# Third down pass of an encoder block: unit 8 of three column groups in half-size products

## The chip, the cores and the metric

The kernel runs on one core of one Trainium2 chip. The metric is device time in microseconds (us). The time before is 2462.04 us, the median of three runs (2459.8 to 2468.41).

## The reference

One layer of a hybrid encoder in float32, with 512 tokens and width 2048. The part that matters here is the channel mixer at its end, and the norm behind it:

```python
x = x + g1 * (merged @ w_out[l])
h2 = rms_norm(x, norm2_w[l]) * (1.0 + sc2) + sh2
ff = (jax.nn.silu(h2 @ w_ffn_gate[l]) * (h2 @ w_ffn_up[l])) @ w_ffn_down[l]   # 5632 -> 2048
x = x + g2 * ff
return rms_norm(x, final_w)
```

`g2` is a row of 2048 gate values, the same for all tokens.

## The kernel before

Every float32 matrix product is made of three matmuls: each operand is split into a high and a low part (`split`: ScalarE copies the high part, VectorE subtracts it to give the low one), and high x high, high x low and low x high are summed in PSUM (`mm3`, lines 188 to 190).

The product with `w_ffn_down` runs over 5632 features, in 11 units of 512 features (4 feature tiles of 128). The 2048 output columns are taken in four groups `cc` of 512. The output of a group is 512 tokens x 512 columns. There are three down passes and a final pass:

- First pass: units 0 and 1, plain (`form2`).
- Second pass (`down_group` with units 2, 3, 4 in products and unit 5 plain), for each `cc`.
- Third pass (the loop near the end): units 6 and 7 in products, units 8 and 9 plain, for each `cc`. In `cc` 0 the two plain units come first (`lead`), in the others last (the `tail`).
- Final pass: unit 10, with the gate `g2` multiplied into its weights, the residual sum, and the final norm, by token tiles.

"In products" means that a unit's 512 x 512 x 512 block is computed by seven half-size products instead of eight, as in Strassen's scheme with Winograd's sums. `wforms` loads two raw weight tiles, makes four sums of 128 x 512 on VectorE (lines 696 to 699), and splits four tiles into the buffers `whl` (one of 128 x 512 and three of 128 x 1024; line 168 on ScalarE, line 170 on VectorE). `sforms` makes the same forms of a unit's activations, which it loads from `ff_d` in DRAM; they lie in one of three `slots` and are used by all four groups. The order of the products is `ORDER = (1, 2, 3, 5, 6, 7, 4)`, or `LATE` for the first unit of some groups. A plain unit (`plain` in `down_group`) splits two raw tiles and needs no sums; its split activations lie in an area `a0` or `a1` (`place`), 128 x 4096 each.

There are five raw buffers (`raw`) and five split buffers (`whl`). A unit in products takes two and four of them, a plain unit two and two. The weight loads go out on SyncE's queue (SP), each when its buffer is free again. The products of a group accumulate in the eight PSUM banks. When the units in products are done, the four banks that only they use go into the accumulator `acc` (lines 1466 to 1480) beside the tail, and the other four behind it (line 1485). `acc` is loaded from `acc_d` at the start of a group, by GpSimd's queue (POOL).

At the end of a group in the third pass, its gated sum is put into `due`, and is made behind unit 7 of the next group (`late`): line 1576 multiplies `acc` by `g2`, line 1577 adds the residual `xr`, each in two instructions of 128 x 1024. For `cc` 0 to 2 the sum is stored to `x2p_d`, and loaded again before the final pass (line 1557); the fourth stays in SBUF. The residual comes from `x2_d`, a DRAM tensor that the pass over `w_out` wrote, and is loaded by POOL group by group (line 1569), with the row of `g2` behind it (line 1570). In `cc` 3 POOL also loads the gate's rows for the final pass (`gf`, line 439, from `rows(wide2[0], g2_d)`), into the buffer of unit 7's forms. Unit 10's activations (`fl`) are loaded by POOL and split behind units 8 and 9 of `cc` 1.

The framework's planner sets the order of the instructions on each engine: by priority, which follows the program's order, and by its own estimate of when each is ready. So an engine's order differs from the program's. `tc.high_priority()` puts instructions forward; `behind` (`tc.keep_in_program_order`) keeps those it wraps in program order among each other. Each engine, and each queue, then works strictly in that order. `bg` holds generators such as `sforms`, which are taken a step further by `pump()` after each unit.

Of the kernel before, what the change touches and what calls it, by code (L numbers as in the profile page):

```python
# [14 lines left out]
F32 = mybir.dt.float32  # L15
# [5 lines left out]
P = 128  # L21
WARM = 12, 14
D = 2048
# [89 lines left out]
def encoder_block(ctx: ExitStack, tc, xp, xT, c, ada1_w, ada2_w, b_ada, norm1_w, w_in, q_norm_w, k_norm_w, bias,  # L113
# [1050 lines left out]

    x2_d = dram.tile([T, D], F32, name="x2d")
    mod["queue"] = nc.sync
# [18 lines left out]
    def residual(cc, g, ssq, eng, x, keep=None):  # L1185
        cs = slice(cc * 512, (cc + 1) * 512)

        def evac(i, b):
            o = io.tile([P, 512], F32, tag="io", name="ro")
            V.tensor_mul(o, b, g[:, cs])  # L1190
            eng.tensor_add(x(i, cc), x(i, cc), o)
            if ssq:
                square(x(i, cc), ssq[i][:, cc:cc + 1])
            if keep is not None:
                t0 = i // 2 * 256 + i % 2
                nc.sync.dma_start(keep[t0:t0 + 255:2, cs], x(i, cc))
        return evac
# [185 lines left out]

    def sforms(j, u):

        big, low = slots[j]
        e, o = (raw_tile("ffe") for _ in range(2))
        for a, r in enumerate((e, o)):
            nc.gpsimd.dma_start(r, ff_d[u][:, a * 1024:(a + 1) * 1024])
        sa = wq.tile([P, 1024], F32, tag="ta", name="sa", bufs=2)  # L1390
        sb = wq.tile([P, 1024], F32, tag="tb", name="sb", bufs=1)
# [125 lines left out]
    f0 = 40  # L1517
    xr = p_e.tile([P, 3072 + 64], F32, tag="s23072", name="xr")
    xo = [xr[:, :2048].rearrange("p (i n) -> p i n", i=NT)]
    fl = p_e.tile([P, 4096 + 64], F32R, tag="s24096", name="fl")  # L1520
    wl = {}
    x2p_d = [dram.tile([P, NT, 512], F32, name=f"x2pd{cc}") for cc in range(3)]
    sq3 = [small.tile([P, 4], F32, tag=f"sq{i}", name=f"sq3{i}", bufs=1) for i in range(NT)]
# [8 lines left out]
    def late(cc):  # L1532
        def behind(u):
            if cc == 0 and u == 8:
                while bg:
                    pump()
            if cc == 1 and u > 7:
                a = u - 8
                xl_pairs.append(ff_pair(10, a, [fl[:, a * 2048 + e * 1024:a * 2048 + (e + 1) * 1024] for e in range(2)],
                                        pin=tc.keep_in_program_order))  # L1540
            if u == 7 and due:
                due.pop()()
            if cc == 3 and u == 6:
# [20 lines left out]

    def factor(cc):
        return xr[:, 2048 + cc % 2 * 512:2560 + cc % 2 * 512]

    def residual_of(cc):
        nc.gpsimd.dma_start(xo[0], x2_d[:, cc * 512:(cc + 1) * 512].rearrange("(i p) d -> p i d", p=P))
        nc.gpsimd.dma_start(factor(cc), g2_d[cc].partition_broadcast(P).rearrange("p o d -> p (o d)"))  # L1570

    def gated_sum(cc, acc):
        to = xo[0] if cc < 3 else x2[3]
        for t in range(2):
            ts = slice(2 * t, 2 * t + 2)
            behind(V.tensor_mul(acc[:, ts], acc[:, ts], factor(cc).unsqueeze(1).to_broadcast([P, 2, 512])))
            behind(V.tensor_add(to[:, ts], xo[0][:, ts], acc[:, ts]))
        if cc < 3:
            nc.gpsimd.dma_start(x2p_d[cc], xo[0])
            residual_of(cc + 1)  # L1580

    residual_of(0)
    for cc in range(4):
        acc = acc_tile()
        nc.gpsimd.dma_start(acc, acc_d[cc])
        down_group(cc, (6, 7), cl, acc, late(cc), () if cc else (8, 9), late=cc > 1,
                   after_lead=cc == 1)
# [87 lines left out]
```

## Time and profile before

| | |
|---|---|
| median of three runs | 2462.04 us |
| profiled execution: its own time, its span | 2466.89 us, 2465.1 us |
| mean granted TensorE clock | 0.998 |
| second down pass, groups cc 1, 2, 3 | 38.86, 38.86, 42.74 us |
| third down pass, groups cc 0 to 3 | 40.20, 40.21, 40.21, 40.20 us |
| final pass, to the end of the span | 52.49 us |

PE is TensorE's matmuls and PEld its weight loads, DVE is VectorE, ACT ScalarE, POOL GpSimd, and SP SyncE. Times in a trace are counted from the start of the span. The stretches in the table begin and end where the timeline of PE shows a group's first matmul. A matmul's row gives 0.28 us for 128 x 256, but matmuls are pipelined: the distance from start to start, 0.11 us in the dense stretches, is what each costs. A wait is written as "who <- for whom: us in total, times, longest".

### The profile page before, as it was taken

How to read it: one execution, taken by the hardware profiler on the slowest of the kernel's cores; microseconds unless marked ns; L12 is line 12 of the kernel's file. 1: busy time of each engine (PE TensorE's matmuls, PEld its weight loads, DVE VectorE, ACT ScalarE, POOL GpSimd, SP SyncE). 2: the span in 40 equal slices, each digit the busy share in tenths (PEclk: the TensorE clock that was granted, in tenths of full speed). 3: DMA queues.
4: the chain of work that ended last, by engine and by line, in shares of the span. 5: the costliest groups of instructions: out<-in, count | busy, mean ns of one | idle time of the engine just before them, and what ended most of it. 6: DMA issues, size and time to landing. Idle time of an engine off the chain costs nothing.

```text
span 2465.1 us, 42367 instructions
## 1 busy us (share of the span) xinstructions
PE 2433.0 (99%) x17327; PEld 2279.4 (92%) x17327; DVE 2007.1 (81%) x2704; ACT 1069.2 (43%) x1466; POOL 150.8 (6%) x255
## 2 busy tenths in 40 slices
PE   8999999999999999999999999999999999999998
PEld 7888888999888888888999999999999998999997
DVE  7995778998677678667899889889899885687877
ACT  5223545544344523337744444444444454433333
POOL 0000000000011111111000000000000000000010
PEclk9999999999999999999999999999999999999999
DMA  9775232455767687867444454444454456546563
GB/s 354 291 261 159 82 98 83 146 180 187 245 206 235 214 297 248 301 204 230 137 154 154 140 163 153 127 156 154 138 171 139 136 189 223 187 155 231 192 246 126
DMA packets 213731, 461.77 MB, mean 187 GB/s; under 512 B 15153, under 2 KB 59553, under 8 KB 204833
## 3 DMA queue, kind: packets, MB, share of 16 engines
q1 hardware_dynamic: 174160, 309.76, 38.6%
q0 software_dynamic: 29872, 132.73, 15.8%
q10 hardware_dynamic: 9504, 16.58, 1.9%
q8 instruction: 136, 2.23, 0.4%
q14 instruction: 59, 0.48, 0.1%
HBM read 412.84 MB, written 46.17 MB: 186 GB/s over the span
## 4 chain that ended last, share of the span: by engine, by line
PE 71%; DVE 14%; issue 8%; DMA 5%; ACT 1%; POOL 0%; DVEq 0%; SPq 0%; POOLq 0%; ACTq 0%
PE mm L190 14%; PE mm L188 14%; PE mm L189 14%; PE S L188 6%; PE S L190 6%; PE S L189 6%; DVE whl L170 3%; PE Y L188 3%; PE Y L189 3%; PE Y L190 2%; DVE raw L524 2%; DMA raw<-in_w_down 2%; PE T L886 1%; DVE g_acc L631 1%; DMA raw<-in_w_in 1%
## 5 line engine op out<-in xcount | busy, mean ns | idle before, releaser
L168 ACT ACTIVATE whl<-raw 128x1024 fp32r<-128x1024 f32 (+1 forms) x483 | 453.7, 943 | 673.9 <-PE mm L190 292.2
L170 DVE TENSOR_TENSOR whl<-raw,whl 128x1024 fp32r<-128x1024 f32 (+1 forms) x483 | 517.5, 1086 | 124.0 <-ACT whl L168 123.7
L168 ACT ACTIVATE whl<-ta 128x1024 fp32r<-128x1024 f32 x124 | 131.4, 1060 | 182.6 <-PE mm L190 112.9
L168 ACT ACTIVATE whl<-tb 128x1024 fp32r<-128x1024 f32 x124 | 131.4, 1060 | 171.7 <-PE S L190 116.5
L170 DVE TENSOR_TENSOR whl<-ta,whl 128x1024 fp32r<-128x1024 f32 x124 | 151.3, 1220 | 41.8 <-ACT whl L168 41.5
L388 DVE SCALAR_TENSOR_TENSOR acc<-mw,cact,acc 128x1024 f32<-128x1024 f32 x124 | 158.8, 1281 | 19.6 <-DMA mw<-in_ada_w 19.3
L170 DVE TENSOR_TENSOR whl<-tb,whl 128x1024 fp32r<-128x1024 f32 x124 | 150.9, 1217 | 5.9 <-ACT whl L168 5.8
L366 POOL DMA_DIRECT2D mw<-in_ada_w x113 | 60.3, 534 | 1357.1 <-DVE acc L388 939.2
L697 DVE TENSOR_TENSOR ta<-raw,ta 128x512 f32<-128x512 f32 x124 | 85.2, 687 | 65.4 <-DMA raw<-in_w_down 27.2
L696 DVE TENSOR_TENSOR ta<-raw 128x512 f32<-128x512 f32 x124 | 85.3, 688 | 36.3 <-DMA raw<-in_w_down 33.8
L188 PE MATMUL mm<-x56h,whl 128*128 128x256 f32 x336 | 92.7, 276 | 0.3 <-DVE c L784 0.2
L189 PE MATMUL mm<-x56l,whl 128*128 128x256 f32 x336 | 92.4, 275 | 0.0
L190 PE MATMUL mm<-x56h,whl 128*128 128x256 f32 x336 | 92.4, 275 | 0.0
L188 PE MATMUL mm<-x3h,whl 128*128 128x256 f32 x320 | 88.1, 275 | 0.5 <-DVE c L782 0.5
L188 PE MATMUL mm<-whl,s 128*128 128x256 f32 x320 | 88.2, 276 | 0.0
L189 PE MATMUL mm<-whl,s 128*128 128x256 f32 x320 | 88.1, 275 | 0.0
L190 PE MATMUL mm<-x3h,whl 128*128 128x256 f32 x320 | 88.0, 275 | 0.0
L190 PE MATMUL mm<-whl,s 128*128 128x256 f32 x320 | 88.0, 275 | 0.0
L189 PE MATMUL mm<-x3l,whl 128*128 128x256 f32 x320 | 88.0, 275 | 0.0
L190 PE MATMUL S<-x56h,whl 128*128 128x256 f32 x320 | 88.0, 275 | 0.0
L188 PE MATMUL S<-x56h,whl 128*128 128x256 f32 x320 | 88.0, 275 | 0.0
L189 PE MATMUL S<-x56l,whl 128*128 128x256 f32 x320 | 88.0, 275 | 0.0
(1879 smaller groups left out, 8909.2 us busy)
## 6 DMA issues: line engine op xcount, KB each, us to landing
raw<-in_w_in SPq DMA_DIRECT2D x133, 512.0 KB, 4.7
mw<-in_ada_w POOLq DMA_DIRECT2D x113, 512.0 KB, 4.5
raw<-in_w_gate SPq DMA_DIRECT2D x92, 512.0 KB, 4.6
raw<-in_w_up SPq DMA_DIRECT2D x88, 512.0 KB, 4.6
raw<-in_w_down SPq DMA_DIRECT2D x88, 512.0 KB, 5.3
raw<-in_ada_w POOLq DMA_DIRECT2D x29, 1024.0 KB, 5.3
raw<-in_w_out SPq DMA_DIRECT2D x48, 512.0 KB, 5.4
ffd<-c SPq DMA_DIRECT2D x10, 1024.0 KB, 4.8
```

The source lines that it names most:

```text
L168: high = pin(S.activation(hi, src, AF.Copy))
L170: latest[:] = [high, pin(eng.tensor_sub(lo, src, hi))]
L188: nc.tensor.matmul(o, lh, rh, start=start, stop=False, **kw)
L189: nc.tensor.matmul(o, lh, rl, start=False, stop=False, **kw)
L190: nc.tensor.matmul(o, ll, rh, start=False, stop=stop, **kw)
L366: mod["queue"].dma_start(w, ada2_w[n * P:(n + 1) * P, :])
L388: behind(V.scalar_tensor_tensor(acc, part, cact[:, k:k + 1], acc, op0=ALU.mult, op1=ALU.add))
L524: V.scalar_tensor_tensor(raw, raw, 1.0, call, op0=ALU.mult, op1=ALU.mult, accum_out=y)
L631: V.tensor_add(acc, acc, b)
L696: V.tensor_sub(t1, b12, b11)
L697: V.tensor_sub(t2_, b22, t1)
L886: nc.tensor.transpose(tp[:, k * P:(k + 1) * P], e[:, k * P:(k + 1) * P], ident)
```

## The change

Unit 8 is computed in products in `cc` 1, 2 and 3, and stays plain in `cc` 0, where it leads. For that its activations are brought into forms once, in `cc` 0 behind unit 9: they are loaded into area `a1` by POOL in one transfer of 1 MB, not into raw buffers, and the sums and the forms' intermediate tiles lie there as well. The forms go into the third slot, which the second pass used for unit 4. What lay in that slot moves: the split activations of unit 10 (`fl`) go to `a1` behind the forms and are loaded by SP's queue; the residual tile `xr` is dropped, and the rows of `g2` get two small buffers.

The gated sum for `cc` 0 to 2 is no longer added on VectorE. The product goes to DRAM with a DMA that adds it to `x2_d` there, in two halves; `x2_d` is now eight tensors of 256 x 512, and the final pass loads it from there. For `cc` 3, VectorE adds into the loaded tile as before. The third gated sum, that of `cc` 2, is made behind unit 8 of `cc` 3 and not behind unit 7, behind the loads of the gate's rows. The weights of the final pass for `cc` 2 go to the third slot, and those for `cc` 3 stay in `a0`.

```diff
-    x2_d = dram.tile([T, D], F32, name="x2d")
+    x2_d = [[dram.tile([256, 512], F32, name=f"x2d{cc}{t}") for t in range(2)] for cc in range(4)]
...
-                nc.sync.dma_start(keep[t0:t0 + 255:2, cs], x(i, cc))
+                nc.sync.dma_start(keep[cc][i // 2][i % 2::2, :], x(i, cc))
...
-    def sforms(j, u):
+    def sforms(j, u, room=None):
...
+        else:
+            e, o, sa, sb = (room[:, n * 1024:(n + 1) * 1024] for n in range(4))
+            nc.gpsimd.dma_start(room[:, :2048], ff_d[u])
+            yield
...
+    def load_x2(to, cc):
+        for t in range(2):
+            nc.gpsimd.dma_start(to[:, 2 * t:2 * t + 2], x2_of(cc, t))
...
+            if cc == 0 and u == 9:
+                forms = sforms(2, 8, p_s.tile([P, 4096 + 64], F32, tag="a1", name="f8"))
+                next(forms)
+                bg.append(forms)
             if cc == 1 and u > 7:
                 a = u - 8
-                xl_pairs.append(ff_pair(10, a, [fl[:, ...] for e in range(2)], pin=tc.keep_in_program_order))
-            if u == 7 and due:
-                due.pop()()
+                if a == 0:
+                    fl.append(p_s.tile([P, 4096 + 64], F32R, tag="a1", name="fl"))
+                xl_pairs.append(ff_pair(10, a, [fl[0][:, ...] for e in range(2)], nc.sync, pin=tc.keep_in_program_order))
...
                 rows(wide2[0], g2_d)
+                load_x2(x2[3], 3)
+            if u == (8 if cc == 3 else 7) and due:
+                due.pop()()
...
                 for c in range(3):
-                    nc.gpsimd.dma_start(x2[c], x2p_d[c])
+                    load_x2(x2[c], c)
...
     def gated_sum(cc, acc):
-        to = xo[0] if cc < 3 else x2[3]
+        f = factors.pop(0).unsqueeze(1).to_broadcast([P, 2, 512])
         for t in range(2):
             ts = slice(2 * t, 2 * t + 2)
-            behind(V.tensor_mul(acc[:, ts], acc[:, ts], factor(cc).unsqueeze(1).to_broadcast([P, 2, 512])))
-            behind(V.tensor_add(to[:, ts], xo[0][:, ts], acc[:, ts]))
+            behind(V.tensor_mul(acc[:, ts], acc[:, ts], f))
+            if cc == 3:
+                behind(V.tensor_add(x2[3][:, ts], x2[3][:, ts], acc[:, ts]))
+            else:
+                nc.gpsimd.dma_start(x2_of(cc, t), acc[:, ts], accum_op=ALU.add)
         if cc < 3:
-            nc.gpsimd.dma_start(x2p_d[cc], xo[0])
-            residual_of(cc + 1)
+            factor_of(cc + 1)
...
-        down_group(cc, (6, 7), cl, acc, late(cc), () if cc else (8, 9), late=cc > 1,
+        down_group(cc, (6, 7, 8) if cc else (6, 7), {9: cl[9]} if cc else cl, acc, late(cc), () if cc else (8, 9), late=cc > 1,
                    after_lead=cc == 1)
...
-        wt = p_s.tile([P, 4096 + 64], F32R, tag=f"a{3 - cc}", name=f"w{cc}")
+        wt = (p_e if cc == 2 else p_s).tile([P, 4096 + 64], F32R, tag="s24096" if cc == 2 else "a0", name=f"w{cc}")
```

More of the change, by code (lines that the diff above doesn't have):

```diff
@@ L1194, in evac @@
             if keep is not None:
-                t0 = i // 2 * 256 + i % 2
-                nc.sync.dma_start(keep[t0:t0 + 255:2, cs], x(i, cc))
+                nc.sync.dma_start(keep[cc][i // 2][i % 2::2, :], x(i, cc))
         return evac
@@ L1382, in __getitem__ @@
             return tuple(Tokens(half(t)[:, :, q]) for t in self.pairs[j])
-    def sforms(j, u):
+    def sforms(j, u, room=None):
         big, low = slots[j]
[L1387 to L1391, printed above, removed]
+        if room is None:
+            e, o = (raw_tile("ffe") for _ in range(2))
+            for a, r in enumerate((e, o)):
+                nc.gpsimd.dma_start(r, ff_d[u][:, a * 1024:(a + 1) * 1024])
+            sa = wq.tile([P, 1024], F32, tag="ta", name="sa", bufs=2)
+            sb = wq.tile([P, 1024], F32, tag="tb", name="sb", bufs=1)
+        else:
+            e, o, sa, sb = (room[:, n * 1024:(n + 1) * 1024] for n in range(4))
+            nc.gpsimd.dma_start(room[:, :2048], ff_d[u])
+            yield
         a11, a21, a12, a22 = e[:, :512], e[:, 512:], o[:, :512], o[:, 512:]
@@ L1517, in encoder_block @@
     f0 = 40
[L1518 to L1522, printed above, removed]
+    fl, wl = [], {}
+    x2_of = lambda cc, t: x2_d[cc][t].rearrange("(i p) d -> p i d", p=P)
+    def load_x2(to, cc):
+        for t in range(2):
+            nc.gpsimd.dma_start(to[:, 2 * t:2 * t + 2], x2_of(cc, t))
     sq3 = [small.tile([P, 4], F32, tag=f"sq{i}", name=f"sq3{i}", bufs=1) for i in range(NT)]
@@ L1536, in behind @@
                     pump()
+            if cc == 0 and u == 9:
+                forms = sforms(2, 8, p_s.tile([P, 4096 + 64], F32, tag="a1", name="f8"))
+                next(forms)
+                bg.append(forms)
             if cc == 1 and u > 7:
                 a = u - 8
-                xl_pairs.append(ff_pair(10, a, [fl[:, a * 2048 + e * 1024:a * 2048 + (e + 1) * 1024] for e in range(2)],
-                                        pin=tc.keep_in_program_order))
-            if u == 7 and due:
-                due.pop()()
+                if a == 0:
+                    fl.append(p_s.tile([P, 4096 + 64], F32R, tag="a1", name="fl"))
+                xl_pairs.append(ff_pair(10, a, [fl[0][:, a * 2048 + e * 1024:a * 2048 + (e + 1) * 1024] for e in range(2)],
+                                        nc.sync, pin=tc.keep_in_program_order))
             if cc == 3 and u == 6:
@@ L1563, in encoder_block, with factor_of @@
     due = []
[L1565 to L1570, printed above, removed]
+    def factor_of(cc):
+        f = p_e.tile([P, 512], F32, tag="g2f", name="g2f", bufs=2)
+        nc.gpsimd.dma_start(f, g2_d[cc].partition_broadcast(P).rearrange("p o d -> p (o d)"))
+        factors.append(f)
     def gated_sum(cc, acc):
-        to = xo[0] if cc < 3 else x2[3]
+        f = factors.pop(0).unsqueeze(1).to_broadcast([P, 2, 512])
         for t in range(2):
             ts = slice(2 * t, 2 * t + 2)
-            behind(V.tensor_mul(acc[:, ts], acc[:, ts], factor(cc).unsqueeze(1).to_broadcast([P, 2, 512])))
-            behind(V.tensor_add(to[:, ts], xo[0][:, ts], acc[:, ts]))
+            behind(V.tensor_mul(acc[:, ts], acc[:, ts], f))
[3 more added lines that the diff above has]
+                nc.gpsimd.dma_start(x2_of(cc, t), acc[:, ts], accum_op=ALU.add)
         if cc < 3:
-            nc.gpsimd.dma_start(x2p_d[cc], xo[0])
-            residual_of(cc + 1)
-    residual_of(0)
+            factor_of(cc + 1)
+    factors = []
+    factor_of(0)
     for cc in range(4):
```

## The prediction

> **What bounds the kernel now.** First the page, for the engines' shares:
>
> ```profile
> PE 2433.0 (99%) x17327; PEld 2279.4 (92%) x17327; DVE 2007.1 (81%) x2704; ACT 1069.2 (43%) x1466; POOL 150.8 (6%) x255
> ```
>
> TensorE is busy 99%, so only less work on it, or fewer of its waits, can shorten the run. Next its waits from 1980 us to the end, where the change lies:
>
> ```profile
> PE S L189 <- DVE whl L170: 0.9, 1, 0.9
> PE S L188 <- ACT whl L168: 0.8, 1, 0.8
> PE mm L189 <- DVE w L170: 0.4, 1, 0.4
> ```
>
> 2.1 us of 485. Third, the table by stretch (columns: stretch, length, busy time of PE, PEld, DVE, ACT, POOL with counts, granted clock, DMA share, GB/s). I cut it where the timeline of PE shows a column group begin. The first three rows are the second down pass's groups cc 1 to 3, the next four the third pass's cc 0 to 3, then the final pass; the last two are a stretch across the third pass's first boundary, and one after a stall:
>
> ```profile
> 2131.33:2170.19 38.86, 38.86 (x350) 38.86 (x349) 27.43 (x36) 14.12 (x15) 1.07 (x2) 1.00 0.49 163
> 2170.19:2209.05 38.86, 38.86 (x350) 38.86 (x349) 29.34 (x39) 14.17 (x15) 2.13 (x4) 1.00 0.50 163
> 2209.05:2251.79 42.74, 41.02 (x350) 40.63 (x349) 36.58 (x46) 19.20 (x21) 5.02 (x9) 0.96 0.71 234
> 2251.79:2291.99 40.20, 40.20 (x362) 40.20 (x361) 30.56 (x40) 15.80 (x17) 1.61 (x3) 1.00 0.58 195
> 2291.99:2332.20 40.21, 40.21 (x363) 40.21 (x362) 34.10 (x42) 14.22 (x15) 2.91 (x5) 1.00 0.60 206
> 2332.20:2372.41 40.21, 40.21 (x362) 40.21 (x361) 32.02 (x40) 12.42 (x13) 2.38 (x4) 1.00 0.53 191
> 2372.41:2412.61 40.20, 40.20 (x362) 40.20 (x361) 29.34 (x32) 14.29 (x15) 5.02 (x9) 1.00 0.84 310
> 2412.61:2465.10 52.49, 42.23 (x206) 36.53 (x204) 41.86 (x80) 16.69 (x43) 0.00 (x0) 0.96 0.24 84
> ...
> 2228.40:2231.60 3.20, 3.20 (x18) 3.20 (x17) 2.39 (x4) 1.06 (x1) 0.53 (x1) 0.50 0.96 330
> ...
> 2266.50:2316.90 50.40, 50.40 (x454) 50.40 (x454) 48.42 (x61) 21.44 (x23) 3.75 (x7) 1.00 0.50 162
> ```
>
> The reader is to see three things. The four groups of the third pass are dense, 40.2 us each. A group of the second pass, which already has the shape that cc 1 to 3 are to get (three units in products, one plain), takes 38.86 us when dense; its fourth took 42.74. And VectorE is busy 48.42 of 50.40 us (96%) across the boundary from cc 0 to cc 1, just where the change adds to it.
>
> **The saving.** A plain unit is 4 feature tiles x 4 token tiles x 2 halves x 3 matmuls = 96; in products it is 7 x 2 x 2 x 3 = 84. cc 1, 2 and 3 lose 12 each, 36 in all. 40.21 / 360 matmuls is 0.1117 us each, so 36 x 0.1117 = 4.02 us; the rows agree, since 3 x (40.21 - 38.86) = 4.05. I take 4.0 us, 0.16% of the time.
>
> **What VectorE gets in return.**
>
> ```profile
> 2295.59 1.21 DVE L170 TENSOR_TENSOR whl<-tb,whl 128x1024 fp32r<-128x1024 f32 x1
> 2296.73 0.68 DVE L170 TENSOR_TENSOR whl<-raw,whl 128x512 fp32r<-128x512 f32 x1
> 2297.33 0.68 DVE L698 TENSOR_TENSOR tb<-raw 128x512 f32<-128x512 f32 x1
> 2297.93 0.68 DVE L699 TENSOR_TENSOR tb<-raw,ta 128x512 f32<-128x512 f32 x1
> 2298.53 1.22 DVE L170 TENSOR_TENSOR whl<-raw,whl 128x1024 fp32r<-128x1024 f32 x1
> ...
> 2301.94 1.21 DVE L1576 TENSOR_TENSOR acc<-acc,xr 128x1024 f32<-128x1024 f32 x1
> ...
> L1577 DVE TENSOR_TENSOR xr<-xr,acc 128x1024 f32<-128x1024 f32 x6 | 7.3, 1222 | 0.1
> ```
>
> Start to start, an operation of 128x1024 holds the engine 1.14 us and one of 128x512 0.60. Weights in forms: 4 sums x 0.60 + 0.60 + 3 x 1.14 = 6.4 us; a plain unit 2 x 1.14 = 2.3. That is +4.1 in each of three groups. Unit 8's activations in forms, once: the same 6.4. Removed: the adds of the first three gated sums, six by 1.14 = 6.8, since the DMA now accumulates; the last sum keeps its adds. Net 12.3 + 6.4 - 6.8 = +11.9 us on VectorE, against 160.8 - 126.0 = 34.8 us that it has free in the four groups. ScalarE's +2 and +4 splits fit into more than 24 us free in each group. So the total fits; the question is the place.
>
> The place is cc 1. TensorE reaches 2310.76 in the old cc 1, the start of unit 8, and the first gated multiplication begins at 2301.94. The fifth product of unit 8 comes 36 matmuls, 4.0 us, later: 2314.8. Before then, from 2301.94, VectorE has 12.9 us for two gated multiplications (2.3), unit 8's four weight sums and its first three splits (2.4 + 0.60 + 2 x 1.14 = 5.3) and the activation forms (6.4): 14.0 us. The evacuations that stand there now move behind unit 8. Short by 1.1 us. Lower bound 0, or below nothing if the queue is better packed than now (it has 2.0 us free in that 50.4 us stretch); upper bound: the forms are put ahead of the boundary. There, the third split of cc 1's first unit ends at 2295.59 + 1.21 = 2296.8, and its product, 12 matmuls behind the row below, starts at 2298.7: ahead by 1.9 us. 6.4 - 1.9 - 2.0 = 2.5 us. I take 1.1, as the forms may be done any time from their load on.
>
> ```profile
> 2297.36 0.28 PE L188 MATMUL S<-whl,s 128*128 128x256 f32 x1
> ...
> 2310.76 0.28 PE L188 MATMUL Y<-whl,a 128*128 128x256 f32 x1
> ...
> 2226.14 0.38 PE L188 MATMUL S<-whl,s 128*128 128x256 f32 x1 [0.84 <-ACT whl L168]
> 2227.40 0.38 PE L189 MATMUL S<-whl,s 128*128 128x256 f32 x1 [0.88 <-DVE whl L170]
> ```
>
> A wait costs more than itself. The second pass's fourth group, which had to fit two sets of activation forms, waited twice for a split, 0.84 and 0.88 us, and then ran 3.2 us at a granted clock of 0.50. It lost 42.74 - 38.86 = 3.9 us, so 2.2 us beyond the two waits. The one expected wait is of their size; I add 1.7 us, since there is one restart and not two. The Trainium skill, "TensorE: Matmul & The Clock Gate", Part 1, has the clock halve only after an idle window of about 3.4 us; by that the 1.7 would be nothing and the forecast 1.7 lower. The trace differs: half clock after waits of 0.9 us, and I go by it.
>
> **Edits that I cost at nothing.** The forms' load: one MB on GpSimd's queue, into area a1 as soon as unit 8's lead is done (2251.79 + 96 x 0.1117 = 2262.5).
>
> ```profile
> 2266.27 0.53 POOL L1585 DMA_DIRECT2D acc<-accd  x1 [6.24 <-DMA accd<-acc]
> 2288.85 0.53 POOL L1314 DMA_DIRECT2D ffr<-ffd  x1 [22.04 <-DVE whl L170]
> ...
> L1314 SPq DMA_DIRECT2D ffr<-ffd x2: 338/338/339, 1977.2 to 1983.1; - x2
> ```
>
> That queue stands still for 22.04 us before 2288.85, so the load goes out by 2267 at the latest; 1 MB took 7.3 us even in the busiest stretch (a row further down), so it has landed by 2275, 36 us before need. It takes none of the weights' raw buffers, unlike the forms in the second pass's fourth group. Unit 10's two loads go to SP's queue: 0.34 us of issue each, and queued behind them are weight loads that wait for the same ring of buffers anyhow. Unit 10's splits must now wait until a1's forms are read; they have until the final pass. The 16 stores into smaller tensors are as many and as long. The gated sums' loads (four of x2, three stores, three reloads) become six accumulates and eight half loads; GpSimd issues for 1.6 to 5.0 us a group, so it has room. Bounds for these together: no gain, as TensorE waits for none of them now; one stall of 2.8 us (1.1 + 1.7) if SP stands behind unit 10's load. I take 0, as its buffers come round in the same order on either queue.
>
> **The end.** The last group is short of DMA:
>
> ```profile
> DMA packets 2787, 10.22 MB, mean 341 GB/s; under 512 B 245, under 2 KB 245, under 8 KB 2145
> ...
> x2pd<-xr POOLq DMA_DIRECT2D x1, 1024.0 KB, 7.3
> gf<-g2d POOLq DMA_DIRECT2D x4, 256.0 KB, 9.8
> ...
> xb<-x2pd POOLq DMA_DIRECT2D x1, 1024.0 KB, 8.6
> ...
> 2390.40 1.60 POOL L439 DMA_DIRECT2D gf<-g2d  x3 [2.52 <-PE S L190]
> ...
> 2399.95 1.23 DVE L1528 TENSOR_TENSOR raw<-raw,gf 128x1024 f32<-128x1024 f32 x1 [4.27 <-DMA gf<-g2d]
> 2422.80 0.48 PE L189 MATMUL mm<-w,fl 128*128 128x512 f32 x1 [0.35 <-DVE w L170]
> ```
>
> (the first four from the DMA view of 2380 to 2410.) VectorE starts the final weights when the gate's rows land, and TensorE waits 0.35 us at 2422.80. The rows' buffer is freed by unit 7 of cc 3, which comes 2 x 1.34 = 2.7 us earlier, while the final pass wants its weights 4.0 us earlier: up to 1.3 us lost. For it: the gated sum's store no longer stands ahead of the rows (three issued at 2390.40, the fourth after 2400), so they should land sooner than 9.8 us; VectorE has 10.9 us free in this group and two adds fewer. I take 0, between -0.4 (the wait goes) and +1.3.
>
> **Sum.** -4.0 + 1.1 + 1.7 + 0 + 0 = -1.2 us. The profiled execution took 2466.89 us, 4.9 above the median of 2462.04; it is within the spread of the runs (2459.8 to 2468.41), so I move the median: 2460.8 us.
>
> **The rivals.**
> 1. All of the new vector work is hidden: the planner puts the forms into free stretches, or the gated multiplications later. For: the second pass's cc 1 and 2 have this shape and are dense, with VectorE at 27.4 and 29.3 of 38.9 us. Against: they have no gated sum and no forms beside them, and 96% is busy here. -4.0: 2458.0, and with the last wait gone 2457.6.
> 2. VectorE cannot catch up, slower than before: behind at cc 1's unit 8, it stays behind, and each of the three groups stalls like the second pass's fourth. Price 3 x 3.9 - 4.0 = +7.6: 2469.6. It decides from a stall of 4.0 / 3 = 1.3 us a group. For: 36.58 of 42.74 us busy (86%) did stall, and cc 1 will have some 34.1 + 4.1 - 2.3 + 3.2 = 39 of 38.9. Against: cc 2 has 32.0 + 1.8 of 38.9, so it recovers 5 us.
> 3. The saving is lost at the end: the DMA engines move 10.22 MB in 30 us there, and the third sum's accumulate reads what it adds to, 1 MB more than the store did, 1 / 0.341 = 3.1 us, in front of the final weights. -4.0 + 3.1, with the last term's +1.3 on top: +0.4, 2462.4. The Trainium skill, "Collectives: The Full Stack", Part 3, has the DMA's add limited by its two source reads; no run here shows an accumulate. Against: the last 1 MB, xb, lands behind the weights at no cost, being read only at 2427.98:
>
> ```profile
> 2427.98 0.69 DVE L1608 TENSOR_TENSOR xb<-xb,ro 128x512 f32<-128x512 f32 x1
> ```
>
> **How the numbers follow.** Forecast 0.52, rival 1 0.22, rival 2 0.12, rival 3 0.14. The forecast's own range is 2457.5 to 2463. The range reaches past rival 1, less 2 us of scatter between runs, and to most of the way to rival 2, whose full price has less than 0.1: 2456 to 2468. 0.3% is 7.4 us, about what a measurement can tell from no change. The whole saving is 4.0, so faster by more takes scatter: 0.04. Slower by more is the worse half of rival 2, and scatter: 0.08. The rest, 0.88, is no change.
>
> **What would show it.** PE counts fall by 36; groups cc 1 to 3 start 38.9 us apart where dense. A wait of TensorE for a split (whl or s) in cc 1 near 2311 to 2316, with a clock of 0.5 behind it, shows the forecast; none shows rival 1; waits in all three groups, rival 2. Waits of the final pass's first 24 matmuls for w or whl of more than 1.5 us show rival 3. The six accumulates should land in less than 20 us and nobody wait for them. I am wrong if SP stands still behind unit 10's loads, or if GpSimd's queue holds up an accumulator's load.

## The result, and the profile after

The changed kernel took 2479.97 us (median of six runs, 2477.71 to 2484.38) where the kernel before took 2462.12 (2459.8 to 2468.41): 1.0067 times as long, with an interval of 1.0056 to 1.0078. The forecast was 2460.8, with a range of 2456 to 2468. The profiled execution of the changed kernel took 2477.71 us (span 2475.8), that of before 2466.89 (span 2465.1); so the two profiles lie 10.8 us apart and explain that much. The other 7 us of the medians' 17.9 are the two profiles' places among their runs: 4.8 above its median before, 2.3 below it after. A part of this may lie ahead of the change: the twenty profiles of this case reach the third pass between 2246.6 us (e15) and 2251.8 (before).

The page's totals, and TensorE's waits from 1980 us to the end, of the changed kernel:

```profile
PE 2433.3 (98%) x17291; PEld 2276.5 (92%) x17291; DVE 2018.9 (82%) x2724; ACT 1077.5 (44%) x1476; POOL 157.5 (6%) x258
```

```profile
PE S L189 <- DVE whl L170: 4.5, 5, 1.8
PE mm L189 <- DVE w L170: 3.4, 1, 3.4
PE mm L189 <- DVE whl L170: 2.2, 2, 1.8
PE S L188 <- ACT whl L168: 1.7, 2, 1.0
PE Y L189 <- DVE whl L170: 0.9, 1, 0.9
PE T L662 <- ACT acc L1494: 0.7, 1, 0.7
```

The 36 matmuls are gone (17,327 to 17,291), and TensorE waits 12.7 us for splits where it waited 2.1. VectorE's total rose by 11.8 us, as the sum had it (11.9). The table by stretch, cut at the third pass's groups cc 0 to 3 and at the final pass:

```profile
2250.43:2290.60 40.17, 38.35 (x328) 38.16 (x327) 30.46 (x40) 16.14 (x19) 1.59 (x3) 0.96 0.57 198
2290.60:2333.47 42.87, 42.87 (x384) 42.73 (x383) 40.80 (x54) 17.27 (x18) 3.67 (x4) 1.00 0.65 191
2333.47:2373.64 40.17, 39.39 (x351) 39.01 (x349) 30.08 (x40) 14.13 (x15) 3.62 (x4) 1.00 0.59 165
2373.64:2413.70 40.06, 39.12 (x351) 38.93 (x349) 30.33 (x36) 11.82 (x13) 7.68 (x11) 1.00 0.78 250
2413.70:2475.80 62.10, 45.09 (x206) 37.44 (x204) 47.05 (x84) 20.45 (x47) 2.72 (x3) 0.91 0.35 111
```

(The cut between cc 0 and cc 1 lies some matmuls early; the two rows are read together.) Against the rows of before: the third pass starts 1.4 us earlier; it takes 163.3 us and not 160.8, so the saving of 4.0 is met by 6.5 of stalls (4.0 in cc 0 and cc 1, 1.3 in cc 2, 1.2 in cc 3); and the final pass takes 62.10 us and not 52.49. -1.4 + 2.5 + 9.6 = 10.7. Nine tenths of the loss lie in the final pass, and there VectorE is busy 47.05 us where it was busy 41.86.

The stall in cc 0, on TensorE and then on VectorE:

```profile
2281.31 0.28 PE L188 MATMUL mm<-whl,s 128*128 128x256 f32 x1
2283.40 0.38 PE L189 MATMUL mm<-whl,s 128*128 128x256 f32 x1 [1.81 <-DVE whl L170]
...
2284.35 0.42 PE L188 MATMUL mm<-whl,s 128*128 128x256 f32 x1
2284.56 0.42 PE L189 MATMUL mm<-whl,s 128*128 128x256 f32 x1
```

```profile
2274.43 0.68 DVE L1397 TENSOR_TENSOR f<-f 128x512 f32<-128x512 f32 x1
...
2276.24 1.21 DVE L170 TENSOR_TENSOR s<-f,s 128x1024 fp32r<-128x1024 f32 x1
...
2282.66 0.68 DVE L170 TENSOR_TENSOR whl<-raw,whl 128x512 fp32r<-128x512 f32 x1
2283.26 1.22 DVE L170 TENSOR_TENSOR s<-f,s 128x1024 fp32r<-128x1024 f32 x1
```

The forms of unit 8's activations (`f`, `s`) stand ahead of the first weight split of unit 7 in cc 0 (2282.66), for which TensorE waits. Behind the wait the matmuls start 0.21 us apart, not 0.11. Now the end, VectorE and GpSimd's queue:

```profile
2392.20 2.35 DVE L1587 TENSOR_TENSOR acc<-acc,g2f 128x1024 f32<-128x1024 f32 x2
2399.97 1.23 DVE L1534 TENSOR_TENSOR raw<-raw,gf 128x1024 f32<-128x1024 f32 x1 [5.42 <-DMA gf<-g2d]
2401.11 0.68 DVE L1475 TENSOR_TENSOR acc<-acc,p 128x512 f32<-128x512 f32 x1
2401.72 3.49 DVE L170 TENSOR_TENSOR whl<-raw,whl 128x1024 fp32r<-128x1024 f32 x3
...
2433.07 1.22 DVE L170 TENSOR_TENSOR w<-raw,w 128x1024 fp32r<-128x1024 f32 x1
```

```profile
2391.79 2.16 POOL L439 DMA_DIRECT2D gf<-g2d  x4 [1.09 <-PE S L190]
...
2403.55 1.22 POOL L1591 DMA_DIRECT2D x2d<-acc  x1 [2.56 <-DVE whl L170]
2414.31 1.23 POOL L1591 DMA_DIRECT2D x2d<-acc  x1 [9.55 <-DMA x2d<-acc]
```

The gate's rows land when they did before (VectorE goes on at 2399.97; before 2399.95). But here unit 9's two splits (the first two of the three at 2401.72; the third is a final weight's) and the evacuation of the banks (L1475 onwards) stand behind the wait, and the last split of the final weights starts at 2433.07, 19.4 us into the final pass. Before, VectorE's timeline had these rows:

```profile
2393.27 1.21 DVE L170 TENSOR_TENSOR whl<-raw,whl 128x1024 fp32r<-128x1024 f32 x1
...
2421.52 1.22 DVE L170 TENSOR_TENSOR w<-raw,w 128x1024 fp32r<-128x1024 f32 x1
```

Unit 9's splits and the evacuation were done by 2395.7, ahead of the wait, and the last split came 8.9 us into the pass.

### The profile page after: what moved, and what is told of

It reads as the page before. It is cut to its first block, busy times and chain, and to the rows that moved or that the text cites. A ratio compares the mean times of both kernels' runs of the same rounds, so it can differ in the third digit from the quotient of the medians.

```text
span 2475.8 us, 42337 instructions
## 1 busy us (share of the span) xinstructions
PE 2433.3 (98%) x17291; PEld 2276.5 (92%) x17291; DVE 2018.9 (82%) x2724; ACT 1077.5 (44%) x1476; POOL 157.5 (6%) x258
## 4 chain that ended last, share of the span: by engine, by line
PE 70%; DVE 16%; DMA 6%; issue 5%; ACT 1%; POOL 0%; DVEq 0%; POOLq 0%; ACTq 0%; SPq 0%
PE mm L190 14%; PE mm L189 14%; PE mm L188 14%; PE S L188 6%; PE S L190 6%; PE S L189 6%; DVE whl L170 4%; DMA raw<-in_w_down 3%; PE Y L188 2%; PE Y L189 2%; PE Y L190 2%; DVE raw L524 2%; PE T L886 1%; DMA ffr<-ffd 1%; DVE g_acc L631 1%
## 5 line engine op out<-in xcount | busy, mean ns | idle before, releaser
L697 DVE TENSOR_TENSOR ta<-raw,ta 128x512 f32<-128x512 f32 x127 | 87.4, 688 | 64.9 <-DMA raw<-in_w_down 32.6
L189 PE MATMUL mm<-whl,s 128*128 128x256 f32 x368 | 102.3, 278 | 2.2 <-DVE whl L170 2.2
L188 PE MATMUL mm<-whl,s 128*128 128x256 f32 x368 | 102.1, 277 | 0.0
L190 PE MATMUL mm<-whl,s 128*128 128x256 f32 x368 | 102.0, 277 | 0.0
```

What stands on the lines that cost most here:

```text
L188: nc.tensor.matmul(o, lh, rh, start=start, stop=False, **kw)
L189: nc.tensor.matmul(o, lh, rl, start=False, stop=False, **kw)
L190: nc.tensor.matmul(o, ll, rh, start=False, stop=stop, **kw)
L697: V.tensor_sub(t2_, b22, t1)
```

## The experiments

Each was timed beside the kernel before, so the ratio counts. "Lost" is the third pass's length over its matmuls at 0.1117 us each; the last column is the final pass to the end of the span. Both are of the one profiled execution, and what is said of "lost" behind e5 shows that it can differ by 3.5 us between executions of the same order. "Long tail" means that `cc` 3 again ends in two plain units.

| run | median us | ratio, interval | lost | final |
|---|---|---|---|---|
| before | 2462.1 | 1 | 0.0 | 52.5 |
| changed | 2480.0 | 1.0067 [1.0056, 1.0078] | 6.5 | 62.1 |
| e1 unit 9 pinned first | 2475.3 | 1.0064 [1.0051, 1.0077] | 7.2 | 61.1 |
| e2 no accumulates | 2480.3 | 1.0072 [1.0060, 1.0085] | 14.7 | 59.7 |
| e4 two rows early | 2477.4 | 1.0059 [1.0045, 1.0073] | 14.1 | 55.9 |
| e5 no forms | 2473.4 | 1.0049 [1.0037, 1.0062] | 10.7 | 59.2 |
| e6 long tail | 2476.7 | 1.0060 [1.0046, 1.0074] | 4.4 | 62.4 |
| e7 long tail, no forms | 2474.5 | 1.0054 [1.0042, 1.0067] | 2.6 | 63.7 |
| e8 no multiplications | 2464.1 | 1.0009 [1.0000, 1.0017] | 5.6 | 51.5 |
| e9 third sum at unit 7 | 2485.2 | 1.0095 [1.0081, 1.0109] | 15.4 | 60.4 |
| e10 gate at the output | 2468.6 | 1.0033 [1.0021, 1.0045] | 4.2 | 55.3 |
| e11 the same, forms later | 2473.2 | 1.0060 [1.0048, 1.0073] | 9.8 | 56.8 |
| e12 no products | 2474.6 | 1.0056 [1.0043, 1.0069] | -0.1 | 62.4 |
| e13 unit 9 before the banks | 2475.2 | 1.0058 [1.0045, 1.0070] | 7.4 | 60.2 |
| e14 no products, rows on ScalarE | 2462.5 | 1.0001 [0.9993, 1.0010] | -0.1 | 51.5 |
| e15 long tail, rows on ScalarE | 2467.1 | 1.0020 [1.0011, 1.0029] | 5.1 | 55.3 |
| e16 gate at three outputs | 2469.9 | 1.0032 [1.0019, 1.0044] | 4.5 | 58.3 |
| e17 the same, no forms | 2474.3 | 1.0046 [1.0033, 1.0060] | 1.7 | 61.9 |
| e18 changed, rows on ScalarE | 2472.5 | 1.0043 [1.0031, 1.0055] | 5.5 | 60.2 |
| e19 no multiplications, no forms | 2461.3 | 1.0001 [0.9993, 1.0010] | 1.4 | 54.0 |

**First, one suspect at a time.**

e1:

```diff
-                hi, lo = wsplit(w_down, 4 * u + 2 * e, 2, c0, 512)
+                hi, lo = wsplit(w_down, 4 * u + 2 * e, 2, c0, 512, pin=<program order where cc 3, u 9>)
...
+  the multiplications by wide2[0] in gated_split pinned behind them
```

> Theory Q (VectorE's queue): in the changed kernel the first gate multiplication of the final weights stands ahead of unit 9's two splits in VectorE's order and waits 5.4 us for the gate's rows; the raw buffers behind it come free late, so the last five weight loads go out 8 to 12 us later than before, and the final pass loses 9.6 us. Here unit 9's splits are held ahead of the multiplications. Q: TensorE's wait of 0.94 us at unit 9 of cc 3 goes, two of the five loads go out about 7 us earlier, the final pass takes 55 to 58 us and not 62.1, the run 2474 to 2477 us. Rival D (DMA): the accumulating transfers and the half loads fill the DMA engines at the end; the order on VectorE is of no account, 2478 to 2482 us. Rival V (VectorE overloaded): the final weights' work simply no longer fits into a group that is 4 us shorter; 2478 to 2482 us.

The splits moved from 2401.72 to 2400.60 only: the planner put the evacuation of the banks ahead of them, with a wait of 2.7 us in it. So this run did not test what it was made for, though its time fell into Q's range; the final pass (61.1) did not. e13 tests it.

e2:

```diff
-                nc.gpsimd.dma_start(x2_of(cc, t), acc[:, ts], accum_op=ALU.add)
```

> The six accumulating transfers are left out (so the first three column groups lack the third pass's part of the sum); all else stays. D: the final weights land earlier, the final pass is shorter by 3 us or more, 2471 to 2477 us. Q and V: nothing on the path waits for them, 2478 to 2482 us.

Without the accumulates it is no faster. But GpSimd's order changed with them: two loads of x2 went ahead of the rows, of which the last went out at 2403.64, and VectorE waited 7.6 us for them. VectorE's order in the third pass stayed the same. It speaks against bandwidth as the cause, and by itself settles little.

e4:

```diff
+                gate01 = <two rows of 512 in the spare of xb's slot>, loaded behind unit 6
-                rows(wide2[0], g2_d)
+                for q in (2, 3): <load row q into wide2[0]>
```

> The gate's rows for column groups 0 and 1 go to the unused end of slot 0's low buffer, which unit 6 frees one and a half units (some 12 us) earlier than unit 7 frees the present place; the same bytes move. Q: the wait of 5.4 us for the rows goes, the raw buffers come round as before the change, the final pass takes 53 to 56 us, the run 2469 to 2473 us. D: no fewer bytes, 2477 to 2482 us. V: VectorE has as much to do, so at most the 5.4 us of waiting are won in part, 2475 to 2479 us.

The wait for the rows went, and another came: VectorE's queue now had the multiplications ahead of unit 8's own splits, where they waited for unit 10's weights.

```profile
DVE raw L1534 <- DMA raw<-in_w_down: 12.9, 4, 4.6
```

The final pass became 6.2 us shorter and the third pass lost 7.6 more.

e5:

```diff
-                forms = sforms(2, 8, p_s.tile([P, 4096 + 64], F32, tag="a1", name="f8"))
...
-                (xh, xl), (wh, wl_) = sx[u][r], w[r]
+                (xh, xl), (wh, wl_) = sx[7 if u == 8 else u][r], w[r]
```

> Unit 8's activations are not loaded and not brought into forms; its products take unit 7's forms instead (so unit 8's part is wrong). Theory F (forms): they stand ahead of unit 7's first split of cc 0 on VectorE and ScalarE, TensorE waits 1.8 us there and then runs at half clock; without them the stretch from cc 0's unit 6 to cc 1's end is dense, 3.5 to 4.0 us less, 2475 to 2477 us, and the final pass stays at 62 us. Against F, if VectorE is at its limit there without them, a wait of 1 us or more stays in cc 0 or cc 1, and less than 2 us are won: 2478 to 2481 us.

cc 0 and cc 1 became dense: the stall of 4.0 us is the forms'. The end did not gain: the order of the queues fell otherwise, and VectorE waited 9.5 us for the rows.

The 4.0 us are one execution's. Twelve profiles keep the forms as the changed kernel has them, with the same order on VectorE, ScalarE and the weight queue in cc 0 and cc 1, and they lost there 1.2 to 4.7 us, with a median of 2.7. The loss follows the time at which VectorE begins the first sum of the forms (L1397), which stands behind a weight sum (L697) that waits for its raw tile. Five of the twelve (some of these runs come further down), counted from the third pass's first matmul:

| run | first sum of the forms, us | lost in cc 0 and cc 1, us | clock behind the longest wait |
|---|---|---|---|
| e9 | 21.2 | 1.2 | 1.00 |
| e18 | 22.6 | 2.6 | 1.00 |
| e8 | 23.9 | 3.9 | 1.00 |
| changed | 24.0 | 4.0 | 0.52 for 3.2 us |
| e4 | 24.7 | 4.7 | 0.50 for 3.4 us |

In all twelve the loss is that time less 20.0 us, to 0.1. So it is VectorE's lateness that is paid, and the slow clock adds nothing to it that can be seen: in e8 the same wait was followed by full clock, and two further waits (0.67 and 0.64 us) took the place of the slow stretch.

```profile
2270.40 0.69 DVE L697 TENSOR_TENSOR ta<-raw,ta 128x512 f32<-128x512 f32 x1 [2.50 <-DMA raw<-in_w_down]
2271.01 0.69 DVE L1397 TENSOR_TENSOR f<-f 128x512 f32<-128x512 f32 x1
...
2280.00 0.38 PE L189 MATMUL mm<-whl,s 128*128 128x256 f32 x1 [1.82 <-DVE whl L170]
...
2280.20:2283.40 3.20, 2.54 (x22) 2.35 (x22) 3.17 (x4) 2.38 (x4) 0.00 (x0) 1.00 0.50 169
```

(All of e8; its third pass begins at 2247.08.)

**Then the end: the tail, the multiplications, the moved sum.**

e6 and e7 (e7 with e5's edit too):

```diff
-        down_group(cc, (6, 7, 8) if cc else (6, 7), {9: cl[9]} if cc else cl, acc, ...
+        down_group(cc, (6, 7, 8) if cc in (1, 2) else (6, 7), {0: cl, 3: {8: cl[9], 9: cl[9]}}.get(cc, {9: cl[9]}), acc, ...
```

> Left out: in cc 3 unit 8 is plain again, with unit 9's activations in place of its own, so cc 1 and cc 2 alone have unit 8 in products (24 matmuls saved, not 36) and cc 3 again ends in two plain units. Theory E (the end): with one plain unit behind the products, VectorE has the evacuation of four banks (8 operations of 0.6 us), the third gated sum, unit 9's splits and the final pass's multiplications and splits in one plain unit's 10.7 us where it had 21.4; the loads and splits of the final weights come late by that. Then the final pass takes 52.5 to 54 us again (changed kernel 62.1) and the time falls from 2480 by 9.6 less 1.3 for the 12 matmuls: 2470 to 2472; the stall in cc 0 and cc 1 (4.0) stays. Theory F (forms of unit 8 alone): no change, 2478 to 2481. Theory W (VectorE overloaded in the whole pass, losses move about): stalls in cc 2 and cc 3 stay, 2475 or more.

> Left out: as in the run before, and unit 8's activation forms too (cc 1 and cc 2 use unit 7's). E and F together: no stall left, third pass dense, 24 matmuls saved: the kernel before less 2.7, 2459 to 2461. W: accumulates, loads or the products' weight sums still stall it: 2465 or more.

Both expectations of E failed: with two plain units at the end the final pass was as long as ever. The wait of VectorE in e6 says why:

```profile
DVE raw L1534 <- DMA gf<-g2d: 14.7, 1, 14.7
```

Here the rows came late, 14.7 us (also in e7). GpSimd's queue now had the third sum's two accumulates ahead of the rows, some 10 us apart.

e8:

```diff
-        if cc != 2:
+        if cc > 3:
             V.tensor_mul(r3, r3, wide2[0][:, cc * 512:(cc + 1) * 512]...)
```

> Left out: the multiplication of the final pass's weights by the gate's row in column groups 0, 1 and 3 (six operations of 128x1024, 6.9 us of VectorE, and with them the wait for the row). Theory Q (VectorE's queue behind the multiplication that waits 5.4 us for the row is the whole of the end): final pass 52.5 to 53.5, 2469 to 2471. Theory E (too much VectorE work in the last unit, of which this is a part): final pass 53.5 to 57, 2471 to 2475. Neither: 2478 to 2481.

```profile
2370.66:2409.52 38.86, 38.86 (x350) 38.86 (x349) 33.03 (x39) 16.41 (x17) 7.69 (x11) 1.00 0.79 274
2409.52:2461.00 51.48, 41.69 (x206) 36.67 (x204) 37.39 (x76) 16.07 (x42) 2.73 (x3) 0.96 0.41 121
```

The whole loss of the end is gone, more than either theory gave, and cc 3 has the 38.86 us that the prediction gave to its shape. VectorE has 9.7 us less to do inside the final pass. The edit takes two things away at once, the work and the wait for the rows. Left over is the third pass's 5.6.

e9:

```diff
-            if u == (8 if cc == 3 else 7) and due:
+            if u == 7 and due:          # ahead of the loads of the rows
                 due.pop()()
```

> Undone: the third gated sum (cc 2's) is again made behind unit 7 of cc 3, ahead of the loads of the gate's rows. E: at most its two multiplications (2.3 us) leave the last 20 us: 2477 to 2480. If the moved sum is the cause of the end's loss: final pass 52.5 to 54 and 2470 to 2472. If the prediction's step on the rows holds (rows land sooner because the sum's store isn't in front of them), undoing it makes the rows later and the time longer: 2481 to 2484.

Slower still by 5 us, and beyond all three ranges: VectorE waited 16.1 us for the rows. So the prediction was right that making the sum behind the rows' loads helps them.

e10 and e11:

```diff
-        if cc != 2:                       (gated_split: weights)
+        if cc > 3:
...
-        if cc == 2:                       (column: output)
+        if True:
```

```diff
(e11 in addition) the sums and splits of sforms(2, 8) under tc.issue_after(<unit 7's last weight split in cc 0>)
```

> The gate's row is multiplied into the output of every column group of the final pass (as it is for column group 2 already), not into the weights of groups 0, 1 and 3: six operations of 128x1024 (6.9 us of VectorE) leave the way to the weights, twelve of 128x512 (7.2 us) come behind the matmuls. Theory Q/E (what counts is that the multiplications stand ahead of the splits on VectorE's queue): final pass 51.5 to 53, as in the run without them, and 2464 to 2467. Theory W (VectorE's amount of work): no better than 2470.

> As the run before, and the forms of unit 8's activations (4 sums, 4 splits) held behind the last weight split of unit 7 in cc 0. Theory F: the stall of 4.0 us at unit 7 of cc 0 goes: 2460 to 2463, even with the kernel before. Rival: the forms then stand with the evacuations in front of unit 6's splits of cc 1, as the prediction's step had it, and one stall of 2.8 to 4 us comes there: 2464 to 2467.

In e10 TensorE ran dense from 2412.69 on; but the norm ended 13.9 us behind its last matmul, not 10.1, since VectorE had 45.03 us to do in the final pass. The loss moved, and a part of it (about 10 us of the 17.9) was won; the time lies between the two theories' ranges. VectorE's work is all still there, behind the matmuls, and the weights came in time: so the amount of it alone does not hold them up, but the part that stands ahead of their splits. In e11 the forms' stall came back bigger, at the start of cc 1, where the prediction had looked for it:

```profile
PE mm L189 <- DVE whl L170: 5.0, 1, 5.0
```

**The accompanying edits alone, and the queue.**

e12:

```diff
-        down_group(cc, (6, 7, 8) if cc else (6, 7), {9: cl[9]} if cc else cl, acc, ...
+        down_group(cc, (6, 7), cl, acc, ...
...  no forms of unit 8; fl in the third slot, w2 in a1, as before
```

> Undone: unit 8 is plain in all four groups, without forms, with unit 10's activations in the third slot as before. What is left are the accompanying edits: accumulating sums, the third sum a unit on behind the gate's rows, eight tensors for x2, unit 10's loads on SP's queue. Theory P (GpSimd's queue: the second half of an accumulate waits some 9 us for the first to land, and the gate's rows stand behind it): VectorE waits 10 us or more for the rows, final pass 58 or more, 2470 to 2476. Theory Q/E (the products and the short tail): dense as before, 2461 to 2463.

e14 (e12 with one more edit), e15 (e6 with it) and e18 (the changed kernel with it):

```diff
-                rows(wide2[0], g2_d)
+                rows(wide2[0], g2_d, nc.scalar)     # the four loads on ScalarE's queue
```

> As the run without products (unit 8 plain everywhere, 2474.6, VectorE waited 13.1 us for the gate's row), but the four loads of the gate's rows for the final pass go out on ScalarE's queue and not on GpSimd's, past the two accumulates; the order on VectorE is the same. Theory P (the rows stand behind the accumulate whose issue waits 8 to 9 us): rows land near 2400, VectorE waits 4 to 6 us, final pass 52.5 to 53.5, 2461 to 2464. Rival D (the accumulates slow the transfers themselves): rows land late all the same, 2470 or more.

> As the run with products of unit 8 in cc 1 and cc 2 alone (left out: unit 8 of cc 3 uses unit 9's activations; 2476.7, VectorE waited 14.7 us for the row), with the rows on ScalarE's queue. P and E together (with the rows out of the queue and two plain units at the end nothing holds the final weights): final pass 52.5 to 53.5, third pass still losing 2.5 to 4.5 to the forms and cc 2, saving 2.7: 2462 to 2465. If the products themselves slow the end: final pass 57 or more, 2468 to 2474.

> The changed kernel, and of it only the four loads of the gate's rows go out on ScalarE's queue (unit 8 stays in products in cc 1 to 3, one plain unit at the end). Theory E (the short tail: evacuation, unit 9's splits, multiplications and splits of the final weights too late in the last plain unit, whenever the rows land): rows land near 2395 to 2400, but the final pass still takes 58 or more, 2474 to 2478. Theory P alone (the rows' time is the whole of the end, as it was without products): final pass 52.5 to 55, 2467 to 2471.

From the third pass on, e12 and e14 have the same order of instructions on VectorE, and so have e6 and e15. e12's timeline, GpSimd and then VectorE:

```profile
2391.43 1.22 POOL L1589 DMA_DIRECT2D x2d<-acc  x1 [3.83 <-DVE whl L170]
2401.09 1.23 POOL L1589 DMA_DIRECT2D x2d<-acc  x1 [8.44 <-issue]
2401.84 2.19 POOL L439 DMA_DIRECT2D gf<-g2d  x3
```

```profile
2407.89 3.49 DVE L1534 TENSOR_TENSOR raw<-raw,gf 128x1024 f32<-128x1024 f32 x3 [13.15 <-DMA gf<-g2d]
```

and e14's, ScalarE's queue and then VectorE:

```profile
2388.64 1.78 ACTq L439 DMA_DIRECT2D gf<-g2d  x4
```

```profile
2393.93 3.50 DVE L1534 TENSOR_TENSOR raw<-raw,gf 128x1024 f32<-128x1024 f32 x3 [0.43 <-DMA gf<-g2d]
```

Every group of e12 is dense, and yet it took 14 us more than before, all in the final pass. The accumulate's second half waited 8.44 us to be issued, and the rows stood behind it. With the rows past it the 14 us are gone, though the accumulates are still there: in this kernel their traffic costs nothing that can be measured, their place in the queue cost everything. Each median in us over that of the kernel before, timed beside it:

| | rows on GpSimd's queue | rows on ScalarE's |
|---|---|---|
| no products of unit 8 | +14.2 (e12) | +0.2 (e14) |
| products in cc 1 and 2, two plain units at the end | +15.2 (e6) | +4.9 (e15) |
| products in cc 1 to 3, one plain unit at the end | +17.9 (changed) | +10.8 (e18) |

In the right column the rest is seen. e15 loses 5.1 us in the third pass, 4.0 of them to the forms, for 2.7 saved; its final pass is still 2.8 us longer than before, so it came out slower than P and E together had it. From e15 to e18 there are 5.9 us more, though 12 matmuls (1.3 us) fewer; what differs is the short tail. e18's final pass is as long as E had it, and its time lies between E's range and P's. e18's final pass, and e15's:

```profile
2410.40:2470.60 60.20, 45.00 (x206) 38.55 (x204) 44.62 (x82) 18.34 (x45) 0.75 (x1) 0.89 0.33 106
```

```profile
2409.94:2465.20 55.26, 43.65 (x206) 37.78 (x204) 40.00 (x78) 16.21 (x42) 1.96 (x3) 0.90 0.33 118
```

VectorE has 44.62 us of work left in the final pass against 40.00. In e18 the rows were there at 2396.30, 3.7 us sooner than in the changed kernel, and still the last split of the final weights started at 2425.51, 15.1 us into the pass (e15: 10.9). Between these two VectorE stood idle 0.34 us in all, so there it is its work that holds the weights:

```profile
2396.30 1.23 DVE L1534 TENSOR_TENSOR raw<-raw,gf 128x1024 f32<-128x1024 f32 x1 [3.84 <-DMA gf<-g2d]
...
2411.76 2.36 DVE L170 TENSOR_TENSOR whl<-raw,whl 128x1024 fp32r<-128x1024 f32 x2 [0.34 <-ACT whl L168]
...
2425.51 1.22 DVE L170 TENSOR_TENSOR w<-raw,w 128x1024 fp32r<-128x1024 f32 x1
```

e13:

```diff
+        made[:] = [wsplit(w_down, 36 + 2 * e, ...) for e in range(2)]   (cc 3: ahead of the evacuation, pinned)
```

> Order on VectorE alone: in cc 3 unit 9's two splits come ahead of the evacuation of the four banks and of the gate's multiplications, so they do not stand behind the wait for the gate's row (in the first such run they were put behind the evacuation and still started at 2400.6). Theory Q: splits at 2394.5 to 2397 instead of 2401.7 to 2405, raw buffers back 5 to 8 us earlier, the last raw load near 2411 instead of 2418, final pass 53 to 57, 2470 to 2475. Theory E (too much VectorE work in the last unit, whatever the order): final pass 59 or more, 2476 to 2480.

This time the order was as meant, and VectorE did not wait for the rows at all:

```profile
2395.88 2.36 DVE L170 TENSOR_TENSOR whl<-raw,whl 128x1024 fp32r<-128x1024 f32 x2 [0.96 <-ACT whl L168]
...
2403.21 1.22 DVE L1534 TENSOR_TENSOR raw<-raw,gf 128x1024 f32<-128x1024 f32 x1
2408.54 1.22 DVE L170 TENSOR_TENSOR w<-raw,w 128x1024 fp32r<-128x1024 f32 x1 [4.11 <-ACT w L168]
...
2433.72 1.23 DVE L170 TENSOR_TENSOR w<-raw,w 128x1024 fp32r<-128x1024 f32 x1
```

Yet the last split came at 2433.72, as in the changed kernel, and the final pass took 60.2. So Theory Q's one change of order does not bring the weights in time. That order has no part is not shown: VectorE now stood idle 7.3 us between 2404 and 2418, waiting for ScalarE's copies, the first of which had waited 10.65 us for a raw weight tile to land. The time, 2475.2, lies between the two theories' ranges.

**Last, whether the saving is there.** e16 is e10 with column groups 0 to 2 at the output; e17 is e16 without the forms; e19 is e8 without the forms.

> The changed kernel with the gate at the output for column groups 0, 1 and 2 of the final pass, and in the weights for group 3 alone. In the run with all four at the output, PE's work was dense to the end but the norm behind it ended 13.9 us later than TensorE's last matmul (10.1 before). Theory Q/E: final pass 51.5 to 52.5, that tail 10 to 11 us: 2464 to 2466. If group 3's two multiplications alone hold the weights up: final pass 55 or more, 2468 or more.

> As the run before, and unit 8's activation forms left out (cc 1 to 3 use unit 7's). If the forms, the rows and the last weights' multiplications are all there is, nothing stalls any more and the saving of 36 matmuls is seen whole: 2457 to 2459. If the products' weight sums cost VectorE too much beside them, cc 2 and cc 3 still lose 1 to 4: 2460 to 2464.

> Left out: the gate's multiplications into the final weights, and unit 8's activation forms (unit 7's are used). If the forms and the multiplications in the short tail are all that eats the saving: third pass dense, 4.0 less than before, 2457 to 2459. If the products' own weight sums (VectorE +4.1 in each group) still stall cc 2 and cc 3: 2460 to 2464.

e16 missed: TensorE was done in time, but the norm ended 14.7 us behind it, no better than in e10. e17 missed too: the accumulates got ahead of the rows again and VectorE waited 8.8 us for them. e19 reached the final pass at 2409.41, 3.2 us earlier than before, with 1.4 us lost in cc 3; then it lost 1.5 in the final pass, where VectorE waited for the last load of x2, once more behind an accumulate:

```profile
DVE xd L1587 <- DMA xd<-x2d: 6.3, 1, 6.3
```

So the saving does appear on TensorE, and of 4.0 us nothing that can be measured was left in the time (1.0001): the interval, 0.9993 to 1.0010, leaves out the 0.9984 that the whole saving would give. No run beat the kernel before.

## Why the prediction was wrong, by its steps

- **The saving, -4.0:** right. 36 matmuls fewer, and a dense group takes 38.86 us (e8).
- **The forms, 1.1 + 1.7:** the forms do stall TensorE (e5, without them: 0), but the place was wrong, and the size came out near by luck. TensorE waited in cc 0 near 2283, not in cc 1 near 2311 to 2316: I wrote that the forms "may be done any time from their load on", and the planner takes them as soon as they land. The twelve profiles with the forms lost 1.2 to 4.7 us there, median 2.7, the changed kernel's 4.0; the 2.8 was worked out for another place. What sets the size is how late VectorE gets to the forms behind a raw weight tile, which the sum did not have. The 1.7 for the slow clock is not shown: the loss is the same with it and without (e8). Held back (e11), the forms cost 7.7 at the start of cc 1.
- **cc 2 and cc 3, nothing:** mis-sized. They lost 1.3 and 1.2 in the changed kernel. VectorE's total over a group fitted; but in cc 2 a weight sum that waited 4.1 us for its raw tile passed the delay on, and in cc 3 unit 9's first split stood behind the wait for the rows (TensorE's 0.9 us on `Y`). The bookkeeping of totals does not exclude such stalls; up to this point the sum would have been 2464.5.
- **Edits at nothing:** this step failed. "GpSimd issues for 1.6 to 5.0 us a group, so it has room" counts how long the queue issues, not how long what stands in it must wait. The two halves of a sum's accumulate went out 9.7 us apart in e12, and everything behind them waited: 14 us in the time. In the changed kernel itself the planner had put the rows ahead of the accumulates; there the same loads on ScalarE's queue, at 2389.16 and not 2391.79, still brought 7 us by the medians (e18); the profiles show 1.9 of them in the final pass, and where the rest lies is not shown. Unit 10's loads on SP's queue and the eight tensors cost nothing (e14 has them), as said.
- **The end, 0 (-0.4 to +1.3):** this step failed, by 9.6 us. It weighed when the rows' buffer comes free, and "10.9 us free in this group". That was time in which VectorE could do nothing: in the old cc 3 it waited 4.3 us for the rows, 4.8 for ScalarE's copies and 1.8 for raw weights, which is all of it, and of the 9.7 us free in the new cc 3, 5.4 are the wait for the rows. What must be done after the last unit in products (evacuation, unit 9's splits, multiplications and splits of the final weights) had 21.4 us of plain matmuls beside it and now 10.7; the rest fell into the final pass, which waits for it. Taking 6.9 us of it away, and the wait for the rows with it (e8), took the loss away; putting the multiplications behind the matmuls kept TensorE dense (e10); unit 9's splits first (e13) did not help; with the rows sooner VectorE was busy without a break and still late (e18); two plain units instead of one, with the rows in time, brought 5.9 (e15 against e18).
- **Rival 1** (all hidden) did not come. **Rival 2** had the sign; but the groups lost 6.5 together, not 11.7, and the end lost more. **Rival 3** had the place; its cause, the accumulate's traffic, falls with e14, which keeps the accumulates and is level with before. On the sentence on the DMA's add the runs have only this: the last sum's halves of 512 KB took 10.4 and 6.3 us to land, the plain store of 1024 KB before 7.3. That the reads are what limits it is not shown.
- **"Nobody wait for them"**, of the accumulates, was wrong: the second half waited 9.55 us for the first. So it is in every run with accumulates: each sum's second half went out 0.31 to 0.33 us after the first had landed. Why it waits, whether by the program's own order or by the queue, is not shown.

What stays open: how the changed kernel's 9.6 us divide between the short tail and the rows, since nearly every edit also changed the planner's order. VectorE's order in the third pass is the same in three pairs: e12 and e14, e6 and e15 (in both only the rows' queue differs, 14.0 and 10.3 us), and the changed kernel and e2. And the 7 us that the medians show beyond the profiles are not located. Nor is it shown why the raw tile ahead of the forms lands later in some executions.

## What to carry to other kernels

Before costing a DMA at nothing, write down what stands behind it on its queue in order, and when the last of these is needed: an issue that waits holds up small loads that have nothing to do with it. When work moves into a group's end, count VectorE's free time from the point where its inputs exist to the point where its results are wanted, not over the group. Here a saving of 0.16% did not pay for 12 us of new work on an engine that feeds the path. And a wait is to be sized from how late the engine behind it is, over several executions: one profile's 4.0 us stood for anything from 1.2 to 4.7.

## What the runs showed of the hardware

The clock: in the changed kernel, behind the wait of 1.81 us at 2283.40 the granted clock was 0.52 for 3.2 us, and behind the 5.0 us in e11 matmuls of 128x256 started 0.21 us apart for 4.9 us. Behind the 3.36 us in the changed kernel's final pass it was 1.00 at once. The first goes against the Trainium skill, "TensorE: Matmul & The Clock Gate", Part 1, by which a wait under about 3.4 us would cost no clock; the last agrees with it. Nor is the length of a wait alone what settles it here: behind e8's 1.82 us the clock stayed at 1.00, and so it did in the changed kernel's second pass (the third line below) behind waits of 0.76 and 0.88 us, whose like before the change (0.84 and 0.88) were followed by half clock. That group took 41.04 us and not 42.74, and from there comes the third pass's earlier start.

```profile
2283.61:2286.81 3.20, 3.20 (x17) 3.20 (x17) 3.17 (x4) 1.77 (x4) 0.00 (x0) 0.52 0.56 176
2432.10:2435.30 3.20, 3.20 (x14) 2.64 (x15) 3.20 (x4) 0.38 (x1) 0.00 (x0) 1.00 0.02 5
...
2209.39:2250.43 41.04, 39.40 (x351) 39.02 (x350) 37.16 (x47) 20.91 (x23) 3.19 (x6) 1.00 0.62 205
```

An accumulate of 512 KB on GpSimd's queue held it 1.21 to 1.28 us for its issue, and the sum's other half went out 6.0 us (e12) to 14.3 us (e15) after it. Four loads of a gate's row, 256 KB each, went out on ScalarE's queue in 1.78 us (e14; 2.75 in e18).
